# RWKV heads of a hybrid layer: the triangular inverse is multiplied into the removal keys and their output weights once per unit, and leaves the state chain

## The chip, the cores and the metric

The kernel runs on one NeuronCore of one Trainium2 chip. The metric is device time in microseconds (us) of one execution, median of several runs. All data is float32; the large products run on float32r pairs (a high and a low part, three products for one).

## What is computed

The reference is one layer of a hybrid trunk on a sequence of 2048 frames and 1024 channels: an RMS norm, one input projection of 4224 columns, three mixers side by side (RWKV-7 with 8 heads of 64, S5, RG-LRU), an output projection, a gated embedding and a last norm. The change touches the RWKV mixer alone. Cut to what matters, its reference is a recurrence over frames for each head:

```python
def step(S, inp):
    r_t, k_t, v_t, kk_t, b_t, d_t = inp
    S = (S * d_t[:, :, None, :]
         - jnp.einsum('bhvk,bhk->bhv', S, kk_t)[..., None] * b_t[:, :, None, :]
         + v_t[..., None] * k_t[:, :, None, :])
    return S, jnp.einsum('bhvk,bhk->bhv', S, r_t)
```

In a chunk of 64 frames the removals (the term with kk and b) depend on one another. Written for the whole chunk, the removed vectors are U = -M P. P is what the chunk's removal keys kk read from the old state and from the chunk's own values. M is the inverse of a unit lower triangular 64x64 matrix, made from the products of kk and b within the chunk and scaled by the norms of kk. U then enters the new state by its keys b and the output by its weights.

## The kernel before, in words

The sequence is worked through in two halves of 1024 frames. For each half there are 33 column tiles of the input projection, each in two blocks of 512 frames; one block is 8 x 3 matmuls of 128x128 by 128x512 (lines L332, L333, L334 in `inproj`, tile `ps_mm`). This is the feed. The RWKV work runs beside it, in 16 units (8 per half): a unit is a head pair, so two heads on the partitions 0 to 63 and 64 to 127, with two times 256 frames, in all 8 chunks of 64 (`NCH`).

A unit goes through three stages, written as Python generators. `rwkv_front` makes the keys and their products (`bk`, `kx`, `gr`, `mt`; matmuls L396, L398, L418 and L461; evictions on ScalarE and VectorE). `rwkv_solve` inverts the triangular matrices: 31 steps of two small VectorE operations (L80, `stmp` and `xs`) on all 32x32 blocks, a block transposition (L491, L497) into `tm`, and two rounds of 32x32 products (L530 and L541, tile `ps_late`), whose second eviction writes the off-diagonal block of `tm`. It also transposes `bk` into `kb` (L504, L506), makes the bonus (L511) and puts the centred values into `uv` (L519, evicted by two ScalarE copies, L523). `rwkv_chain` walks through the chunks, 4 steps of two chunks each, and carries the state.

One step of the chain before is three products in a row, each with an eviction behind it: (1) L570, `kx` times `uv`, gives P, which VectorE copies to `pt` (L577); (2) L585, `tm` times `pt`, gives U, evicted with a minus sign into `uv` by VectorE for one head and ScalarE for the other; (3) L592, `kb` times `uv`, is added to the state copy `sn` (L575, ScalarE) and scaled by VectorE into the next step's `uv`. Two products for the output (L581 from the old state, L603 from `uv` with the weights `gr`) go to `ps_y` beside them. The last step ends in a group norm (L611) and a store to `Yd`.

The order on TensorE (PE) is the order in which a loop at the end of the stage takes from the generators, and PE works strictly in that order. One tick of this loop takes 9 or 10 feed matmuls (`CHUNK_MM`), then one piece each of the chain, the solve and the front, up to their next `yield`; the number yielded says how many ticks that stage pauses. A front may begin every 15 ticks (`INTERVAL`). The other engines' orders are set by a list scheduler, in which chain, solve and front have the priorities 100, 50 and 0 (`PR_C`, `PR_S`, `PR_F`). The PSUM tiles matter too: `ps_prep` has two buffers, used by the front, by the normalised input's transposes (L319) and by L511; `ps_late` and `ps_chain` have one each.

After both halves the pools of this stage are closed, and the output projection (L922 to L924, `o1a`) and the S5 mixer begin. Their first loads (`st` from `w_out`, `st32` from `s5_a_re` and `s5_a_im`, L975) are issued on the one DMA queue of SyncE (SP), in order behind the last stores of the stage (`Yd` L356, `Gd` L707).

Of the kernel before, what the change touches and what calls it, by code (L numbers as in the profile page):

```python
# [12 lines left out]
AF = mybir.ActivationFunctionType  # L13
# [4 lines left out]
P = 128  # L18
# [4 lines left out]
C = 64  # L23
# [21 lines left out]
def hymba_layer(ctx: ExitStack, tc: tile.TileContext, x, p, norm_g, w_in,  # L45
# [83 lines left out]
    POOL.update((tag, rl) for tag in ("kx", "gr", "tm", "kb", "uv", "dl"))  # L129
    POOL.update((tag, rz) for tag in ("pt", "sn", "sp"))  # L130

# [338 lines left out]

    def rwkv_solve(n, v, mt, inv, bk, r):
        def wt(tag, shape=None, bufs=1):
            return pool_of(tag).tile(shape, F32, tag=tag, name=tag, bufs=bufs)
# [10 lines left out]
        for st in range(31):  # L484
# [4 lines left out]
            sub(xs[:, 0:ni, st + 1:32], xs[:, 0:ni, st + 1:32], tmp[:, 0:ni, 0:n])  # L489
        tn = wt("stmp", [P, 8, 32], 2).rearrange("p i (c q) -> p i c q", q=4)  # L490
        V.transpose(out=tn.rearrange("p i c q -> p i (c q)"), in_=xs)  # L491
        tm = wt("tm", [P, NCH, C], 2)
        for h in range(2):
            G.memset(tm[64 * h + 32:64 * h + 64, :, 0:32], 0.0)
            for bl in range(2):
                g = slice(64 * h + 32 * bl, 64 * h + 32 * bl + 32)
                V.transpose(out=tm[g, :, 32 * bl:32 * bl + 32], in_=tn[g].rearrange("p i c q -> p c i q"))  # L497

# [28 lines left out]
        for c in range(NCH):  # L527
            for h in range(2):
                o = 64 * h
                T.matmul(out=psc[o + 32:o + 64, 32 * c:32 * c + 32], lhsT=mt[o:o + 32, c, 32:64],  # L530
                         rhs=tn[o:o + 32, :, c], start=True, stop=True, tile_position=(o, o + 32))
        qn = wt("stmp", [P, 8, 32], 2)
# [5 lines left out]
        for c in range(NCH):  # L538
            for h in range(2):
                o = 64 * h  # L540
                T.matmul(out=psd[o:o + 32, 32 * c:32 * c + 32], lhsT=qn[o + 32:o + 64, c],  # L541
                         rhs=tm[o + 32:o + 64, c, 32:64], start=True, stop=True, tile_position=(o + 32, o))
        for h in range(2):
            hs = slice(64 * h, 64 * h + 32)
            act(tm[hs, :, 32:64], psd[hs, 0:256].rearrange("p (c t) -> p c t", t=32), AF.Copy, scale=-1.0)
        yield 1
        return tm, kb, uv, bon

    def rwkv_chain(pair, half, q, q_, gd):
        kx, gr, mt, inv, bk, r, dl, tm, kb, uv, bon = q_  # L550
        heads = [slice(0, 64), slice(64, 128)]
# [13 lines left out]
        for st in range(NS):  # L565
            cs = slice(st, NCH, NS)
            ps = psum.tile([P, 4, 2, C], F32, tag="chain", name="ps_chain", bufs=1)
            for j, c in enumerate((st, st + NS)):
                for h, hs in enumerate(heads):
                    T.matmul(out=ps[hs, 0, j], lhsT=kx[:, c, h], rhs=uv[:, c, h], start=True, stop=True,  # L570
                             tile_position=(0, 64 * h))
            if st > 0:
                sn = wt("sn", [P, 2, C], 2)
                for h, hs in enumerate(heads):
                    A.copy(out=sn[hs], in_=uv[hs, cs, h])  # L575
            pt = wt("pt", [P, 2, C])
            V.tensor_copy(out=pt, in_=ps[:, 0])  # L577
            yield W_C
            for c in (st, st + NS):
                for h, hs in enumerate(heads):  # L580
                    T.matmul(out=psy[hs, c * C:(c + 1) * C], lhsT=uv[hs, c, h], rhs=kx[hs, c, 2], start=(c == 0), stop=False,  # L581
                             tile_position=(64 * h, 64 * h), skip_group_check=True)
            for j, c in enumerate((st, st + NS)):
                for h, hs in enumerate(heads):
                    T.matmul(out=ps[hs, 1, j], lhsT=tm[hs, c], rhs=pt[hs, j], start=True, stop=True,  # L585
                             tile_position=(64 * h, 64 * h))
            ts(uv[heads[0], cs, 0], ps[heads[0], 1], -1.0, ALU.mult)
            act(uv[heads[1], cs, 1], ps[heads[1], 1], AF.Copy, scale=-1.0)
            yield 1
            for j, c in enumerate((st, st + NS)):  # L590
                for h, hs in enumerate(heads):
                    T.matmul(out=ps[hs, 2, j], lhsT=kb[:, c, hs], rhs=uv[:, c, h], start=True, stop=True,  # L592
                             tile_position=(0, 64 * h))
            sp = wt("sp", [P, 2, C])
            add(sp, ps[:, 2], sn)
            if st + 1 < NS:
# [260 lines left out]
    def solve_stage():  # L857
        for n, (half, pair, q) in enumerate(units):
            while len(fronts) <= n:
                yield 0  # L860
            yield from need(2, half, pair)
            v = load_z(2, q, zds[half][pair])
            f = fronts[n]
            solved.append(f + (yield from rwkv_solve(n, v, *f[2:6])))
            if n % 8 == 7 and half + 1 < NH:
                while len(chained) < n:
                    yield 0
                nxt[half + 1].append(fetch_x(half + 1, 1))
# [546 lines left out]
```

## Time and profile before

| what | value |
|---|---|
| median of 3 runs | 1825.19 us (1819.2 to 1825.2) |
| the profiled execution | 1823.06 us, of which the span from first to last instruction is 1821.3 us |
| mean granted TensorE clock in it | 0.989 |
| busy: PE matmul, VectorE, ScalarE, GpSimd | 96%, 71%, 53%, 2% of the span |
| DMA | 184.71 MB, mean 101 GB/s |
| feed and RWKV stage | from the start to about 1156.7 us of the span |

The profile is of one execution. PE is the matmul engine, PEld its weight loads, DVE is VectorE, ACT is ScalarE, POOL is GpSimd, SP issues DMAs. A row of a timeline gives start and duration in us; matmuls overlap in time, so what one of them costs is read from the distance between starts. A float32 matmul of the program stands in the trace as two instructions; a float32r one (the feed) as one.

### The profile page before, as it was taken

The page shows a single profiled execution, that of the slowest core. Times are in us where ns is not written, and L with a number is a line of the kernel's source. Part 1 is how long each engine was busy: PE and PEld are TensorE (multiplying, and loading weights), DVE is VectorE, ACT ScalarE, POOL GpSimd, SP SyncE. Part 2 cuts the span into 40 slices and gives each one's busy share as a digit, 9 for nine tenths or more (in the row PEclk, how much of TensorE's full clock was granted, in tenths as well). Part 3 has the DMA queues.
Part 4 walks back from the last instruction along what each step waited for, and adds up shares of the span by engine and source line. Part 5 has one row for each costly group of instructions (what it writes and reads, how often), then busy time and mean ns, then how long its engine had stood idle before and what let it go on. Part 6 is the DMA issues. An engine that isn't in the chain of part 4 may idle for free. (4 is left out here: it accounts for less than half of the span.)

```text
span 1821.3 us, 30173 instructions
## 1 busy us (share of the span) xinstructions
PE 1747.5 (96%) x11212; PEld 1346.6 (74%) x11212; DVE 1287.9 (71%) x3219; ACT 968.8 (53%) x1857; POOL 43.7 (2%) x105
## 2 busy tenths in 40 slices
PE   5999999999998999999999999899999999999997
PEld 4877777777676777777776767678888778888886
DVE  6279788688887439888688885786875685555554
ACT  5345864575757445665558565666763452232222
POOL 1000000000000000000000000000000000000000
PEclk9999999999999999999999999999999999999999
DMA  4332323222223233123222121742334893223220
GB/s 147 116 108 79 93 78 99 90 61 77 83 71 100 82 116 112 52 86 101 82 80 67 51 69 38 197 142 98 110 105 119 221 311 143 85 92 110 78 73 35
DMA packets 214620, 184.71 MB, mean 101 GB/s; under 512 B 59253, under 2 KB 182474, under 8 KB 214474
## 3 DMA queue, kind: packets, MB, share of 16 engines
q1 hardware_dynamic: 214474, 182.79, 32.5%
q8 instruction: 88, 1.44, 0.3%
q14 instruction: 58, 0.48, 0.1%
HBM read 121.73 MB, written 59.83 MB: 100 GB/s over the span
## 5 line engine op out<-in xcount | busy, mean ns | idle before, releaser
L332 PE MATMUL ps_mm<-xh,whi 128*128 128x512 f32 x1056 | 463.0, 438 | 0.9 <-ACT whi L192 0.7
L333 PE MATMUL ps_mm<-xh,wlo 128*128 128x512 f32 x1056 | 416.3, 394 | 0.8 <-DVE wlo L80 0.8
L334 PE MATMUL ps_mm<-xl,whi 128*128 128x512 f32 x1056 | 416.5, 394 | 0.0
L332 PEld LDWEIGHTS ps_mm<-xh,whi 128*128 128x128 f32 x1056 | 200.0, 189 | 79.1 <-issue 31.3
L333 PEld LDWEIGHTS ps_mm<-xh,wlo 128*128 128x128 f32 x1056 | 200.6, 190 | 46.6 <-issue 13.0
L334 PEld LDWEIGHTS ps_mm<-xl,whi 128*128 128x128 f32 x1056 | 200.0, 189 | 45.2
L80 DVE TENSOR_TENSOR stmp<-xs,ms 128x60 f32<-128x60 f32 (+24 forms) x496 | 103.3, 208 | 11.6
L80 DVE TENSOR_TENSOR xs<-xs,stmp 128x60 f32<-128x60 f32 (+24 forms) x496 | 102.7, 207 | 11.5
L923 PE MATMUL ps_mm<-woh,yl 128*128 128x512 f32 x256 | 103.1, 403 | 2.0 <-DVE yl L98 2.0
L922 PE MATMUL ps_mm<-woh,yh 128*128 128x512 f32 x256 | 102.4, 402 | 0.5 <-ACT yh L101 0.4
L924 PE MATMUL ps_mm<-pgl,hh 128*128 128x512 f32 x256 | 101.1, 395 | 0.3 <-DVE pgl L80 0.3
L924 PE MATMUL ps_mm<-wol,yh 128*128 128x512 f32 x256 | 101.3, 396 | 0.0
L923 PE MATMUL ps_mm<-pgh,hl 128*128 128x512 f32 x256 | 101.0, 394 | 0.0
L922 PE MATMUL ps_mm<-pgh,hh 128*128 128x512 f32 x256 | 100.8, 394 | 0.0
L80 DVE TENSOR_TENSOR wlo<-wraw,whi 128x512 fp32r<-128x512 f32 x132 | 88.5, 683 | 14.0 <-ACT whi L192 13.6
L101 ACT ACT_TABLE_LOAD x74 | 94.9, 1283 | 1.3
L101 ACT ACTIVATE ftg<-ps_mm 128x512 f32<-128x512 f32 x32 | 19.1, 598 | 135.4 <-PE ps_mm L924 135.4
L98 DVE SCALAR_TENSOR_TENSOR z<-ps_mm,pc,z 128x511 f32<-128x511 f32 x48 | 35.8, 745 | 69.9 <-ACT z L101 69.8
L192 ACT CAST whi<-wraw 128x512 fp32r<-128x512 f32 x132 | 77.9, 614 | 0.7 <-DMA wraw<-in_w_in 0.2
L98 DVE SCALAR_TENSOR_TENSOR e<-ftg,e 128x1024 f32<-128x1024 f32 x16 | 19.6, 1226 | 78.1 <-ACT ftg L101 78.1
L101 ACT ACTIVATE uv<-ps_chain 64x128 f32<-64x128 f32 x64 | 17.4, 272 | 97.9 <-DVE uv L93 97.2
L101 ACT ACTIVATE z<-ps_mm,dc 128x512 f32<-128x512 f32 x48 | 32.8, 682 | 66.3 <-PE ps_mm L334 66.2
(332 smaller groups left out, 3535.9 us busy)
## 6 DMA issues: line engine op xcount, KB each, us to landing
wraw<-in_w_in SPq DMA_DIRECT2D x132, 256.0 KB
zd<-z SPq DMA_DIRECT2D x48, 256.0 KB
yr<-Yd SPq DMA_DIRECT2D x16, 512.0 KB
Hd<-ht SPq DMA_DIRECT2D x16, 512.0 KB
hr<-Hd SPq DMA_DIRECT2D x16, 512.0 KB
xr<-in_x SPq DMA_DIRECT2D x16, 512.0 KB
out<-e SPq DMA_DIRECT2D x16, 512.0 KB
st<-in_w_out SPq DMA_DIRECT2D x12, 512.0 KB
```

Source lines behind the costliest of these rows:

```text
L80: V.tensor_tensor(out=out, in0=a, in1=b, op=op)
L98: V.scalar_tensor_tensor(out=out, in0=a, scalar=s, in1=b, op0=op0, op1=op1)
L101: A.activation(out=out, in_=in_, func=func, scale=scale, bias=bias)
L192: A.copy(out=hi[:, ks], in_=raw)
L332: T.matmul(out=ps, lhsT=hi[:, k], rhs=xh, start=(k == 0), stop=False)
L333: T.matmul(out=ps, lhsT=lo[:, k], rhs=xh, start=False, stop=False)
L334: T.matmul(out=ps, lhsT=hi[:, k], rhs=xl, start=False, stop=(k == KD - 1))
L922: T.matmul(out=ps, lhsT=a_h[:, k], rhs=b_h[k][:, ns], start=(ends[0] and k == 0), stop=False)
L923: T.matmul(out=ps, lhsT=a_l[:, k], rhs=b_h[k][:, ns], start=False, stop=False)
L924: T.matmul(out=ps, lhsT=a_h[:, k], rhs=b_l[k][:, ns], start=False, stop=(ends[1] and k == nk - 1))
```

## The change

The solve stage now ends with one more piece, and the chain has two products in a row. With M in `tm`, the solve stage multiplies M into the removal keys (`kb`, 16 matmuls of 64x64 by 64x64) and into their output weights (`gr`, 16 more), line L553 after the change; both are written back in place, with a minus sign, by four ScalarE evictions of 64 partitions x 512. The chain then writes P itself into `uv` where U stood (VectorE for one head, ScalarE for the other), and the next product takes it with the new `kb` and `gr`. The products L581 are issued with L570 (L586 with L582 after the change), since P overwrites the state that they read; `pt` is gone. For these products M is needed in the other orientation, so the transposes behind the 31 steps change: three over 128 partitions x 256 in place of one such and four over 32 x 256, and the off-diagonal block is made at another place of `tm`.

```diff
-        tn = wt("stmp", [P, 8, 32], 2).rearrange("p i (c q) -> p i c q", q=4)
-        V.transpose(out=tn.rearrange("p i c q -> p i (c q)"), in_=xs)
         tm = wt("tm", [P, NCH, C], 2)
+        for bl in range(2):
+            V.transpose(out=tm[:, :, 32 * bl:32 * bl + 32].rearrange("p c (i q) -> p i c q", q=4), in_=xs)
+        t1 = wt("stmp", [P, 8, 32], 2)
+        V.transpose(out=t1, in_=tm[:, :, 32:64])
         for h in range(2):
-            G.memset(tm[64 * h + 32:64 * h + 64, :, 0:32], 0.0)
-            for bl in range(2):
-                g = slice(64 * h + 32 * bl, 64 * h + 32 * bl + 32)
-                V.transpose(out=tm[g, :, 32 * bl:32 * bl + 32], in_=tn[g].rearrange("p i c q -> p c i q"))
+            G.memset(tm[64 * h:64 * h + 32, :, 32:64], 0.0)
...
-                T.matmul(out=psd[o:o + 32, 32 * c:32 * c + 32], lhsT=qn[o + 32:o + 64, c],
-                         rhs=tm[o + 32:o + 64, c, 32:64], start=True, stop=True, tile_position=(o + 32, o))
+                T.matmul(out=psd[o + 32:o + 64, 32 * c:32 * c + 32], lhsT=t1[o + 32:o + 64, c],
+                         rhs=qn[o + 32:o + 64, c], start=True, stop=True, tile_position=(o + 32, o + 32))
...
         yield 1
-        return tm, kb, uv, bon
+
+        for ps, of in ((plate(), lambda hs, h: kb[hs, :, hs]), (pprep(), lambda hs, h: gr[hs, :, h])):
+            for c in range(NCH):
+                for h in range(2):
+                    hs = slice(64 * h, 64 * h + 64)
+                    T.matmul(out=ps[hs, c * C:(c + 1) * C], lhsT=tm[hs, c], rhs=of(hs, h)[:, c], start=True, stop=True,
+                             tile_position=(64 * h, 64 * h))
+            for h in range(2):
+                hs = slice(64 * h, 64 * h + 64)
+                act(of(hs, h), ch(ps)[hs], AF.Copy, scale=-1.0)
+        yield 1
+        return kb, uv, bon
...
+            for c in (st, st + NS):
+                for h, hs in enumerate(heads):
+                    T.matmul(out=psy[hs, c * C:(c + 1) * C], lhsT=uv[hs, c, h], rhs=kx[hs, c, 2], start=(c == 0), stop=False,
+                             tile_position=(64 * h, 64 * h), skip_group_check=True)
             if st > 0:
                 sn = wt("sn", [P, 2, C], 2)
                 for h, hs in enumerate(heads):
                     A.copy(out=sn[hs], in_=uv[hs, cs, h])
-            pt = wt("pt", [P, 2, C])
-            V.tensor_copy(out=pt, in_=ps[:, 0])
+            V.tensor_copy(out=uv[heads[0], cs, 0], in_=ps[heads[0], 0])
+            A.copy(out=uv[heads[1], cs, 1], in_=ps[heads[1], 0])
             yield W_C
-            for c in (st, st + NS):
-                for h, hs in enumerate(heads):
-                    T.matmul(out=psy[hs, c * C:(c + 1) * C], lhsT=uv[hs, c, h], rhs=kx[hs, c, 2], start=(c == 0), stop=False,
-                             tile_position=(64 * h, 64 * h), skip_group_check=True)
             for j, c in enumerate((st, st + NS)):
                 for h, hs in enumerate(heads):
-                    T.matmul(out=ps[hs, 1, j], lhsT=tm[hs, c], rhs=pt[hs, j], start=True, stop=True,
-                             tile_position=(64 * h, 64 * h))
-            ts(uv[heads[0], cs, 0], ps[heads[0], 1], -1.0, ALU.mult)
-            act(uv[heads[1], cs, 1], ps[heads[1], 1], AF.Copy, scale=-1.0)
-            yield 1
-            for j, c in enumerate((st, st + NS)):
-                for h, hs in enumerate(heads):
-                    T.matmul(out=ps[hs, 2, j], lhsT=kb[:, c, hs], rhs=uv[:, c, h], start=True, stop=True,
+                    T.matmul(out=ps[hs, 1, j], lhsT=kb[:, c, hs], rhs=uv[:, c, h], start=True, stop=True,
                              tile_position=(0, 64 * h))
```

Three places of the order, first on PE. A chain step before, between the feed's own rows (`ps_mm`); `uv` holds the state and the values, `ps_chain` the step's products:

```order
L570 MATMUL ps_chain<-uv,kx 64x64 x4
L332 MATMUL ps_mm<-xh,whi 128x512
...
L334 MATMUL ps_mm<-xl,whi 128x512
L581 MATMUL ps_y<-kx,uv 64x64 x4
L585 MATMUL ps_chain<-pt,tm 64x64 x4
L332 MATMUL ps_mm<-xh,whi 128x512
...
L334 MATMUL ps_mm<-xl,whi 128x512
L592 MATMUL ps_chain<-uv,kb 64x64 x4
L603 MATMUL ps_y<-gr,uv 64x64 x4
```

The same step after the change (L582, L586, L597, L608 are L570, L581, L592, L603):

```order
L582 MATMUL ps_chain<-uv,kx 64x64 x4
L586 MATMUL ps_y<-kx,uv 64x64 x4
L332 MATMUL ps_mm<-xh,whi 128x512
...
L334 MATMUL ps_mm<-xl,whi 128x512
L597 MATMUL ps_chain<-uv,kb 64x64 x4
L608 MATMUL ps_y<-gr,uv 64x64 x4
```

The step has two pieces where it had three; the output product from the old state moved up to the first of them.

The end of a solve on PE after the change, in a unit where a front's products (L461) fall in the same tick; L542 is the 32x32 product that was L541:

```order
L542 MATMUL ps_late<-stmp 32x32 x16
L332 MATMUL ps_mm<-xh,whi 128x512
...
L334 MATMUL ps_mm<-xl,whi 128x512
L553 MATMUL ps_late<-kb,tm 64x64 x16
L553 MATMUL ps_prep<-gr,tm 64x64 x16
L461 MATMUL ps_prep<-kx,bk 128x128 x8
```

Before the change the solve ended with the first of these rows. The two rows of L553 are new, and L461 uses the buffers of `ps_prep` behind the second of them.

The four new evictions on ACT, in one of these units:

```order
L101 ACTIVATE kk<-zk,pc 128x256 x2
L101 ACTIVATE kb<-ps_late 64x8x64 x2
L101 ACTIVATE sq<-kk 128x512
L101 ACTIVATE gr<-ps_prep 64x8x64 x2
L466 COPY mt<-ps_prep 32x256
L466 COPY mt<-ps_prep 32x4x32
```

None of the rows of `kb` and `gr` was there before; here a piece of the next front (`sq`) stands between them, and the evictions of L461's products (`mt`) come behind them.

The end of the stage on SP, before:

```order
L104 DMA st<-in_w_out 128x1024 x2
L356 DMA Yd<-rst 128x2x128 x2
L975 DMA st_12706<-in_s_a_re 32x64
L707 DMA Gd<-g_12650 128x512
L975 DMA st_12706<-in_s_a_re 32x64
L975 DMA st_12706<-in_s_a_im 32x64 x2
L104 DMA st<-in_w_out 128x1024 x3
```

And after, where L980 is L975 and L712 is L707; the last `Yd<-rst` store stands 13 rows further up and isn't among these:

```order
L104 DMA st<-in_w_out 128x1024
L980 DMA st_12898<-in_s_a_re 32x64 x2
L980 DMA st_12898<-in_s_a_im 32x64
L712 DMA Gd<-g_12842 128x512
L980 DMA st_12898<-in_s_a_im 32x64
L104 DMA st<-in_w_out 128x1024
```

The last store of the RWKV stage and most weight loads moved ahead of the last gate store; one of the four small loads still stands behind it.

More of the change, by code (lines that the diff above doesn't have):

```diff
@@ L129, in hymba_layer @@
     POOL.update((tag, rl) for tag in ("kx", "gr", "tm", "kb", "uv", "dl"))
-    POOL.update((tag, rz) for tag in ("pt", "sn", "sp"))
+    POOL.update((tag, rz) for tag in ("sn", "sp"))
     def pool_of(tag):
@@ L469, in rwkv_front, with rwkv_solve @@
         return kx, gr, mt, inv, bk, r, dl
-    def rwkv_solve(n, v, mt, inv, bk, r):
+    def rwkv_solve(n, v, gr, mt, inv, bk, r):
         def wt(tag, shape=None, bufs=1):
@@ L530, in rwkv_solve @@
                 T.matmul(out=psc[o + 32:o + 64, 32 * c:32 * c + 32], lhsT=mt[o:o + 32, c, 32:64],
-                         rhs=tn[o:o + 32, :, c], start=True, stop=True, tile_position=(o, o + 32))
+                         rhs=tm[o:o + 32, c, 0:32], start=True, stop=True, tile_position=(o, o + 32))
         qn = wt("stmp", [P, 8, 32], 2)
@@ L540, in rwkv_solve @@
                 o = 64 * h
-                T.matmul(out=psd[o:o + 32, 32 * c:32 * c + 32], lhsT=qn[o + 32:o + 64, c],
-                         rhs=tm[o + 32:o + 64, c, 32:64], start=True, stop=True, tile_position=(o + 32, o))
+                T.matmul(out=psd[o + 32:o + 64, 32 * c:32 * c + 32], lhsT=t1[o + 32:o + 64, c],
+                         rhs=qn[o + 32:o + 64, c], start=True, stop=True, tile_position=(o + 32, o + 32))
         for h in range(2):
-            hs = slice(64 * h, 64 * h + 32)
-            act(tm[hs, :, 32:64], psd[hs, 0:256].rearrange("p (c t) -> p c t", t=32), AF.Copy, scale=-1.0)
+            hs = slice(64 * h + 32, 64 * h + 64)
+            act(tm[hs, :, 0:32], psd[hs, 0:256].rearrange("p (c t) -> p c t", t=32), AF.Copy, scale=-1.0)
         yield 1
-        return tm, kb, uv, bon
+        for ps, of in ((plate(), lambda hs, h: kb[hs, :, hs]), (pprep(), lambda hs, h: gr[hs, :, h])):
[9 more added lines that the diff above has]
+        return kb, uv, bon
     def rwkv_chain(pair, half, q, q_, gd):
-        kx, gr, mt, inv, bk, r, dl, tm, kb, uv, bon = q_
+        kx, gr, mt, inv, bk, r, dl, kb, uv, bon = q_
         heads = [slice(0, 64), slice(64, 128)]
@@ L575, in rwkv_chain @@
                     A.copy(out=sn[hs], in_=uv[hs, cs, h])
-            pt = wt("pt", [P, 2, C])
-            V.tensor_copy(out=pt, in_=ps[:, 0])
+            V.tensor_copy(out=uv[heads[0], cs, 0], in_=ps[heads[0], 0])
+            A.copy(out=uv[heads[1], cs, 1], in_=ps[heads[1], 0])
             yield W_C
-            for c in (st, st + NS):
-                for h, hs in enumerate(heads):
-                    T.matmul(out=psy[hs, c * C:(c + 1) * C], lhsT=uv[hs, c, h], rhs=kx[hs, c, 2], start=(c == 0), stop=False,
-                             tile_position=(64 * h, 64 * h), skip_group_check=True)
             for j, c in enumerate((st, st + NS)):
                 for h, hs in enumerate(heads):
-                    T.matmul(out=ps[hs, 1, j], lhsT=tm[hs, c], rhs=pt[hs, j], start=True, stop=True,
-                             tile_position=(64 * h, 64 * h))
-            ts(uv[heads[0], cs, 0], ps[heads[0], 1], -1.0, ALU.mult)
-            act(uv[heads[1], cs, 1], ps[heads[1], 1], AF.Copy, scale=-1.0)
-            yield 1
-            for j, c in enumerate((st, st + NS)):
-                for h, hs in enumerate(heads):
-                    T.matmul(out=ps[hs, 2, j], lhsT=kb[:, c, hs], rhs=uv[:, c, h], start=True, stop=True,
+                    T.matmul(out=ps[hs, 1, j], lhsT=kb[:, c, hs], rhs=uv[:, c, h], start=True, stop=True,
                              tile_position=(0, 64 * h))
             sp = wt("sp", [P, 2, C])
-            add(sp, ps[:, 2], sn)
+            add(sp, ps[:, 1], sn)
             if st + 1 < NS:
@@ L863, in solve_stage @@
             f = fronts[n]
-            solved.append(f + (yield from rwkv_solve(n, v, *f[2:6])))
+            solved.append(f + (yield from rwkv_solve(n, v, *f[1:6])))
             if n % 8 == 7 and half + 1 < NH:
```

## The prediction, made before the run

> **What bounds the kernel now.** I read the page, then the busy time by stage, then the waits of PE, then single intervals of the timeline. Engines and stages first (columns: window, its length, busy time with instruction count of PE, PEld, DVE, ACT and POOL, granted clock, DMA share, GB/s):
>
> ```profile
> span 1821.3 us, 30173 instructions
> PE 1747.5 (96%) x11212; PEld 1346.6 (74%) x11212; DVE 1287.9 (71%) x3219; ACT 968.8 (53%) x1857; POOL 43.7 (2%) x105
> ...
> 0.00:1156.70 1156.70, 1108.74 (x8322) 825.90 (x8322) 865.39 (x2523) 689.24 (x1398) 22.33 (x69) 0.99 0.29 87
> ...
> 100.00:560.00 460.00, 450.77 (x3514) 333.13 (x3511) 381.26 (x1142) 286.75 (x583) 7.03 (x19) 0.99 0.28 83
> ...
> 690.00:1110.00 420.00, 409.13 (x3404) 301.14 (x3403) 351.68 (x1075) 253.51 (x512) 3.67 (x12) 1.00 0.25 75
> ```
>
> The change lies wholly in the first 1156.7 us. In the two stretches where RWKV units run, PE is idle for 460.0 - 450.8 = 9.2 and 420.0 - 409.1 = 10.9 us, about 2%. DVE is at 83%, ACT at 60 to 62%. PE is the bound there: a product that is added to it costs its full time, and a wait that disappears can give back no more than these idle stretches. Which waits they are (waits of PE up to 1160 us and from 560 to 600 us; us in total, times, longest):
>
> ```profile
> PE ps_prep L461 <- DVE gr L80: 3.2, 2, 2.5
> PE ps_chain L592 <- ACT uv L101: 2.9, 6, 0.8
> PE ps_y L581 <- DVE rst L80: 2.4, 3, 1.4
> PE ps_chain L570 <- DVE uv L80: 1.0, 2, 0.9
> ...
> PE ps_prep L319 <- DVE xl L98: 5.7, 4, 3.1
> ```
>
> The state chain is hardly waited for: L570, L581 and L592, the three places where a step takes up an eviction, cost 6.3 us together over 64 steps. Nine feed matmuls between two pieces of the chain cover its evictions. The chain is no critical path that could be shortened; its third product only takes PE time.
>
> **The change part by part.** What a small group costs on PE is read from the starts of the feed matmuls around it.
>
> ```profile
> 522.57 0.39 PE L334 MATMUL ps_mm<-xl,whi 128*128 128x512 f32 x1
> 522.88 0.45 PE L570 MATMUL ps_chain<-uv,kx 128*64 128x64 f32 x8
> 523.26 0.50 PE L332 MATMUL ps_mm<-xh,whi 128*128 128x512 f32 x1
> 523.60 0.39 PE L333 MATMUL ps_mm<-xh,wlo 128*128 128x512 f32 x1
> 523.83 0.40 PE L334 MATMUL ps_mm<-xl,whi 128*128 128x512 f32 x1
> ...
> 589.40 0.39 PE L334 MATMUL ps_mm<-xl,whi 128*128 128x512 f32 x1
> 589.72 0.45 PE L581 MATMUL ps_y<-kx,uv 64*64 64x64 f32 x8
> 590.00 0.40 PE L585 MATMUL ps_chain<-pt,tm 64*64 64x64 f32 x8
> 590.33 0.50 PE L332 MATMUL ps_mm<-xh,whi 128*128 128x512 f32 x1
> 590.67 0.39 PE L333 MATMUL ps_mm<-xh,wlo 128*128 128x512 f32 x1
> ...
> 1077.66 0.39 PE L334 MATMUL ps_mm<-xl,whi 128*128 128x512 f32 x1
> 1077.98 0.45 PE L570 MATMUL ps_chain<-uv,kx 128*64 128x64 f32 x8
> 1078.36 1.15 PE L519 MATMUL ps_late<-cen,zv 64*64 64x64 f32 x32
> 1079.43 0.50 PE L332 MATMUL ps_mm<-xh,whi 128*128 128x512 f32 x1
> 1079.77 0.40 PE L333 MATMUL ps_mm<-xh,wlo 128*128 128x512 f32 x1
> ```
>
> Undisturbed feed starts lie 0.23 apart (523.60 to 523.83). From L334 over a gap to the L333 behind it is two such steps, 0.46. With 8 small instructions in the gap it is 523.60 - 522.57 = 1.03, a delay of 0.57; with 16 it is 590.67 - 589.40 = 1.27, a delay of 0.81. So 8 instructions cost 0.24, 0.030 each, and the interruption of the feed itself 0.57 - 0.24 = 0.33. With 8 + 32 it is 2.11, a delay of 1.65, where 40 x 0.030 + 0.33 = 1.53 would be due: the missing 0.12 stands at the change of shape, since from L570 (128 rows) to the next start is 0.38, from L581 to L585 (both 64 rows) 0.28. I take 0.10 for such a change.
>
> 1. Removed: L585, 64 groups of 8 instructions: 64 x 0.24 = -15.4 us.
> 2. Added: 32 products per unit, 64 instructions in the trace; 16 x 64 x 0.030 = +30.7 us. They have exactly the shape of L585 and L519.
> 3. Interruptions: counted in the order of PE, the feed is broken 285 times before and 266 times after, since a step takes two ticks and not three, while the solve takes one more and its pieces now less often fall together with one of the chain. 19 x 0.33 = -6.3 us.
> 4. L586 now follows L582 in one group, with a change of shape inside it: 64 x 0.10 = +6.4 us (0 if the switch hides elsewhere).
>
> PE alone thus has 30.7 + 6.4 - 15.4 - 6.3 = +15.4 us more, between +9 and +17.
>
> At this place the Trainium skill speaks for the change: TensorEngine Tiling (Array Packing), section Key Properties, says that changing the tiling mode drains the TensorE. The trace agrees (0.33 for an interruption, 0.10 for a change of shape within one); by that rule alone, without the products, the edit would gain the 6.3 us and lose the 6.4.
>
> 5. A new wait. The order of PE shows `ps_prep` products of L461 in the same tick behind the new ones in 10 of the 16 units. `ps_prep` has two buffers: the new product takes one, the first four products of L461 the other, and the next four need the first again, so they wait for the evictions of `gr`, which stand on ACT behind those of `kb`. What an ACT eviction of this size costs and how late it comes:
>
> ```profile
> L523 ACT COPY uv<-ps_late 64x512 f32<-64x512 f32 x32 | 18.5, 579 | 16.4 <-PE ps_late L519 16.1
> ...
> L461 PE MATMUL ps_prep<-kx,bk 64*128 64x128 f32 x512 | 56.4, 286 | 3.4 <-DVE gr L80 3.2 <-PE ps_late L541 0.2
> ...
> 407.77 1.15 PE L519 MATMUL ps_late<-cen,zv 64*64 64x64 f32 x32 [0.65 <-ACT kb L506]
> ...
> 409.68 0.63 ACT L101 ACTIVATE lth<-lth 128x512 f32<-128x512 f32 x1
> 410.34 1.17 ACT L523 COPY uv<-ps_late 64x512 f32<-64x512 f32 x2
> ```
>
> When the `kb` products end, PE has the 32 instructions for `gr` (0.95) and four of L461 (56.4 / 64 = 0.88, with 0.1 for the shape): 1.93 us. ACT needs four evictions, 4 x 0.579, and about 0.1 of latency: 2.42. So PE waits at least 0.5 us. Late evictions add to it: here L519 ended at 408.92 and its eviction began 1.42 later, behind a table load and an activation. Most begin at once, but in ACT's new order other work stands between the `kb` and `gr` evictions in five of the ten units. I take 1.1 us: 10 x 1.1 = +11, between +5 and +25. Behind the waiting L461 stand the feed itself and, on ACT and DVE, the evictions of that front piece.
>
> 6. Chain waits: the one at L581 goes (-2.4); those at L592 and L570 have the same cover of nine feed matmuls, and the evictions are of the same size (64 x 128 on each engine). A new order inside: P may overwrite the state only after L586 and the `sn` copies; both end before the copy would start anyway. I take -2.4, between -5 and +3.
> 7. VectorE and ScalarE.
>
> ```profile
> L577 DVE COPY pt<-ps_chain 128x128 f32<-128x128 f32 x64 | 18.0, 281 | 23.2 <-PE ps_chain L570 22.9
> L497 DVE STREAM_TRANSPOSE tm<-stmp 32x256 f32<-32x256 f32 x64 | 27.8, 435 | 1.2
> ```
>
> DVE loses one of two evictions per step, 18.0 us, and four transposes per unit for two more of the same free size, 27.8 - 32 x 0.435 = 13.9 us: 32 us of 865 in the stage. DVE is not the bound; of the waits on it above (3.2 and 5.7) I take half, -4, between -9 and 0. ACT gains 64 evictions x 0.579 = 37 us at about 61% load: nothing but what item 5 counts.
>
> 8. The end of the stage. The last group norm product (L611) has 33 feed matmuls behind it before and 114 after. What stands there now:
>
> ```profile
> 1156.28 0.39 PE L334 MATMUL ps_mm<-xl,whi 128*128 128x512 f32 x1
> 1161.66 0.28 PE L1008 MATMUL ps_prep<-ident,st 32*128 32x32 f32 x1 [4.99 <-DMA st<-in_s_a_re]
> ...
> 1156.81 0.89 SPq L356 DMA_DIRECT2D Yd<-rst  x2
> ...
> 1158.43 0.37 SPq L707 DMA_DIRECT2D Gd<-g  x1
> 1158.84 0.44 SPq L975 DMA_DIRECT2D st<-in_s_a_re  x1
> 1159.33 0.89 SPq L975 DMA_DIRECT2D st<-in_s_a_im  x2
> ```
>
> SP holds the small loads back behind the last `Yd` store, and that store comes early after the change. But in the new order of SP one of the four `st` loads still stands behind the last `Gd` store, which needs the end of the feed; it moves up by three issues at most, about 1 us, and the weights, now loaded earlier, save some of the slow start behind it. -3, between -6 and 0.
>
> Sum: 15.4 + 11 - 2.4 - 4 - 3 = +17. The profiled execution took 1823.06 us (span 1821.3), 2.1 below the median of the runs and inside their spread; 1823.06 + 17 = 1840.
>
> **The rivals.** *Waits fall more than the products cost (faster).* If the DVE work that goes and the shorter chain took away the waits whole, that is 6.3 (chain), 3.2 and 5.7 (DVE) and 5 at the end, 20 us, against 9 (item 1 to 4 at its low end) and the least new wait, 5: 1823 - 6 = 1817, and with hidden waits inside busy PE time perhaps 1812. For it: DVE at 83% is close behind PE. Against: a sum of idle PE time so small. It decides where products cost under 0.02 us each. Chance 0.09.
>
> *The balance (no change).* Products at the low end of +9, the new wait at +5, gains of -9: 1828. Chance 0.21.
>
> *The clock (slower than forecast).* PE loses its clock behind poorly filled stretches (columns: window, length, PE busy, granted clock, DMA share, GB/s):
>
> ```profile
> 510.30:513.70 3.40, 2.18 (x44) 1.00 0.09 10
> 513.70:517.10 3.40, 3.40 (x16) 0.50 0.55 173
> ```
>
> PE worked 2.18 of 3.40 us here, part of it in 32x32 products, and ran at 0.50 for the next 3.40 us: 1.7 us lost. The new tick is 1.9 us of 64x64 products, 1.8 of L461 and the wait between, about 5 us without feed; if each of the ten lost 1.7 us, that is 17 more: 1857. Against: 64x64 products run in pairs on both halves of the rows, and long ticks without a wait kept the clock. Chance 0.12. The Trainium skill, TensorE: Matmul & The Clock Gate, section on the HAM clock gate, says that the gate looks at PE's activity in free-running windows of 3413 ns; the trace agrees in the 3.40 us steps.
>
> *The chain is not shorter in time.* Fronts begin every 15 ticks whatever the chain takes, and in PE's order the fronts' L418 stand at the same feed positions (288, 420, 561, 711, ...) before and after. This is part of the forecast: the shorter chain ends a unit earlier, but starts the next no sooner.
>
> **How the numbers follow.** Forecast 1840 with chance 0.58; the clock 0.12; the balance 0.21; faster 0.09. The range takes in the lower bound of the balance at about 1826 and the clock case at 1857. 0.5% is 9.1 us, about what a measurement of this kernel can tell from no change; slower by more is forecast and clock, 0.70.
>
> **What would show it.** L553 as 1024 instructions with some 32 us between feed starts; waits of L461 for ACT `gr`, about 1 us each in ten units; L577 and L585 gone; PE idle time near 1157 down to about 4 us; no stretch in which the chain is waited for. It is wrong if the stage ends at 1157 us or before (now 1156.7, forecast about 1176), or if L461 does not wait.

## The result, and the profile after

The changed kernel takes 1889.65 us (median of 4 runs, 1887.37 to 1892.36) against 1823.2 before: a ratio of 1.0368 with a 95% interval of 1.034 to 1.0396. It is slower, as forecast, but by 66 us where 17 were forecast, and outside the range.

The top of the page of the changed kernel, and then its windows view, cut at the last feed matmul (same columns as before):

```profile
span 1885.6 us, 31245 instructions
PE 1782.0 (95%) x11724; PEld 1383.8 (73%) x11724; DVE 1270.8 (67%) x3123; ACT 1005.5 (53%) x1920; POOL 44.0 (2%) x105
```

```profile
0.00:1217.50 1217.50, 1138.43 (x8834) 858.31 (x8834) 852.05 (x2430) 729.37 (x1464) 22.62 (x69) 0.97 0.28 84
1217.50:1885.60 668.10, 643.53 (x2891) 525.49 (x2890) 418.77 (x694) 276.11 (x457) 21.37 (x36) 0.98 0.39 124
```

The stage ends at 1217.5 where it ended at 1156.7: 60.8 us of the 64.3 by which the span grew. In it PE is idle 1217.5 - 1138.4 = 79.1 us (before 1156.7 - 1108.7 = 48.0), 31 more. Its busy time grew by 29.7. Part of that is work at half clock: the trace's clock records show PE busy for 59.8 us at a granted clock of 0.5 in this stage, before 23.9. Counted as half lost, the difference is 18.0 us. The other 11.8 are work at full clock. So 31 us are waits, 18 the clock, 12 the work. The prediction's sum had, in this stage, 11 for new waits less 6.4 for old ones, nothing for the clock, and 15.4 for the work.

The waits of PE up to 1230 us (us in total, times, longest):

```profile
PE ps_prep L461 <- DVE bk L80: 20.6, 7, 6.6
PE ps_mm L332 <- ACT la L101: 11.0, 4, 6.4
PE ps_prep L319 <- DVE xt L93: 8.4, 5, 2.9
PE ps_prep L461 <- ACT gr L101: 5.7, 7, 2.2
PE ps_mm L669 <- ACT li L101: 4.8, 2, 4.2
...
PE ps_prep L1013 <- DMA st<-in_s_a_re: 4.5, 1, 4.5
...
PE ps_prep L553 <- ACT nrow L420: 3.2, 1, 3.2
```

L461 waits for `gr` on ScalarE, as forecast, with 5.7 us. But the first line was not in the trace of before and is in no step of the prediction: L461, the front's own products, comes to PE before VectorE has made their input `bk`. The second and the fifth line are waits for ScalarE's evictions of `la` and `li`, gates of the RG-LRU mixer whose products stand in the feed. They were small before:

```profile
PE ps_mm L664 <- ACT li L101: 0.5, 1, 0.5
PE ps_mm L332 <- ACT la L101: 0.2, 1, 0.2
```

These 15 us more are in no step of the prediction either. Of the runs below, no_products has them too (11.5 and 4.8), without one new product, and bk_wait_5 less (5.0 and 0.9); but `la` is as long in gate_late_two_ticks (12.9), where L461 is late. What holds up these two evictions isn't shown.

One place of the first kind, in rows of PE, ACT and DVE (start, duration, in brackets the idle time ahead):

```profile
795.95 1.15 PE L553 MATMUL ps_late<-kb,tm 64*64 64x64 f32 x32
...
798.09 0.47 ACT L101 ACTIVATE ta<-ps_prep,dc 128x256 f32<-128x256 f32 x1
798.45 1.19 ACT L101 ACTIVATE kb<-ps_late 64x512 f32<-64x512 f32 x2
799.64 0.57 ACT L420 COPY nrow<-ps_prep 2x512 f32<-2x512 f32 x1
800.27 1.97 PE L553 MATMUL ps_prep<-gr,tm 64*64 64x64 f32 x32 [3.17 <-ACT nrow L420]
802.57 1.18 ACT L101 ACTIVATE gr<-ps_prep 64x512 f32<-64x512 f32 x2
...
803.77 1.28 ACT L101 ACT_TABLE_LOAD   x1
805.06 0.47 ACT L101 ACTIVATE ta<-ps_prep,dc 128x256 f32<-128x256 f32 x1
805.57 0.69 DVE L98 SCALAR_TENSOR_TENSOR b<-ta,kk 128x512 f32<-128x512 f32 x1
805.57 0.60 ACT L101 ACTIVATE km<-ta,dc 128x256 f32<-128x256 f32 x1
...
808.71 0.69 DVE L98 SCALAR_TENSOR_TENSOR bk<-b,einv 64x512 f32<-64x512 f32 x1
808.82 3.37 PE L461 MATMUL ps_prep<-kx,bk 64*128 64x128 f32 x16 [6.58 <-DVE bk L80]
...
812.12 0.79 PE L332 MATMUL ps_mm<-xh,whi 128*128 128x512 f32 x1
```

The front's `nrow` and the second halves of its `ta` and `km` stand on ScalarE behind the new evictions (and a table load), `bk` comes after them, and PE stands still for 3.17 and 6.58 us with no feed in between. The new evictions are not what makes `bk` late, though: at the same place in the order PE waits 7.46 us for `bk` in no_products and 6.01 in no_evictions (both below), which have none of them. PE runs at half clock here: the 32 instructions for `gr` take 1.97 where those for `kb` took 1.15, and 16 of L461 take 3.37 where they took 1.71 before the change (at 458.18).

Why L461 is early is told by the order, not by the trace. The second half of a front stands in the code behind `while len(chained) < n - 1: yield 0`, a gate that the end of a chain opens. The shorter chain opens it earlier. In the order of PE the fronts' L418 stand where they stood (but for one of sixteen), but L461 moved up: in the first half its first tick in a front stood at feed matmul 642, 780, 960, 1098, 1272, 1404 before (third to eighth unit), and stands at 612, 750, 900, 1050, 1194, 1335 now. From L418 to L461 it was 69 to 120 feed matmuls in these units, and now is 36 to 51. In the first two units of each half nothing moved: L461 stands 36 to 42 behind L418 in both kernels, and there it doesn't wait for `bk`. No chain runs beside these fronts yet. So the distance alone doesn't make the wait; that it depends on what else the engines have to do is likely, but not shown.

### The profile page after: what moved, and what is told of

It is laid out like the page before. It is cut to its first block, busy times and chain, and to the rows that moved or that the text cites. A ratio compares the mean times of both kernels' runs of the same rounds, so it can differ in the third digit from the quotient of the medians.

```text
span 1885.6 us, 31245 instructions
## 1 busy us (share of the span) xinstructions
PE 1782.0 (95%) x11724; PEld 1383.8 (73%) x11724; DVE 1270.8 (67%) x3123; ACT 1005.5 (53%) x1920; POOL 44.0 (2%) x105
## 5 line engine op out<-in xcount | busy, mean ns | idle before, releaser
L461 PE MATMUL ps_prep<-kx,bk 64*128 64x128 f32 x512 | 68.3, 307 | 26.9 <-DVE bk L80 20.6
L461 PEld LDWEIGHTS ps_prep<-kx,bk 64*128 64x128 f32 x512 | 60.2, 208 | 34.4 <-issue 13.1
```

The lines of the kernel that those rows point to most:

```text
L461: T.matmul(out=ps[:, q * P:(q + 1) * P], lhsT=bk[hs, c].rearrange("p a t -> p (a t)"), rhs=kx[hs, c, h:3:2 - h], start=True, stop=True)
```

## The experiments

Theory A: the early gate costs the time; L461 reaches PE before `bk`, and the clock falls behind the holes (a hole is a wait in which PE stands still). Rival B: the new products and their evictions do it by themselves. The order of a kernel is summed up by two distances in feed matmuls: from a front's L418 to its L461 (third to eighth unit of each half), and from its last L461 to the next front's first product L396 (number of the 14 places below 24, the turn of the halves left out). Ratios are to the kernel before, run beside it.

| kernel | us | ratio, 95% interval | L418 to L461 | close L396 |
|---|---|---|---|---|
| before | 1823.2 | 1 | 63 to 120 | 2 |
| the change | 1889.65 | 1.0368 (1.034 to 1.0396) | 36 to 51 | 0 |
| no_products | 1850.26 | 1.0167 (1.0151 to 1.0183) | as the change | 0 |
| no_evictions | 1868.86 | 1.0268 (1.0248 to 1.0289) | as the change | 0 |
| gate_late | 1863.21 | 1.0228 (1.0209 to 1.0247) | 72 to 147 | 6 |
| gate_late_no_products | 1813.15 | 0.9953 (0.9924 to 0.9982) | as gate_late | 6 |
| gate_late_no_evictions | 1850.03 | 1.0145 (1.013 to 1.016) | as gate_late | 6 |
| gate_late_two_ticks | 1877.24 | 1.0293 (1.0275 to 1.031) | 87 to 153 | 6 |
| before_bk_wait_0 | 1894.35 | 1.0389 (1.0373 to 1.0404) | 27 to 57 | 0 |
| bk_wait_5 | 1834.12 | 1.0064 (1.0047 to 1.0081) | 72 to 111 | 2 |
| bk_wait_5_no_products | 1793.61 | 0.9841 (0.9821 to 0.9861) | as bk_wait_5 | 2 |
| bk_wait_5_split | 1827.58 | 1.0033 (1.0016 to 1.0051) | as bk_wait_5 | 2 |
| bk_wait_6 | 1869.51 | 1.0266 (1.0238 to 1.0294) | 90 to 135 | 8 |
| before_bk_wait_5 | 1872.17 | 1.0273 (1.025 to 1.0296) | 90 to 159 | 10 |
| gate_late_front_pause | 1853.91 | 1.0184 (1.0163 to 1.0205) | 72 to 126 | 0 |
| before_bk_wait_5_front_pause | 1853.29 | 1.0186 (1.016 to 1.0213) | 75 to 138 | 0 |
| before_front_pause | 1815.12 | 0.9969 (0.9956 to 0.9982) | 63 to 120 | 0 |
| bk_wait_5_split_front_pause | 1827.64 | 1.0044 (1.0024 to 1.0065) | 72 to 111 | 0 |

### Gate and products, each with and without

gate_late puts the gate back near its old place; the front's gate then asks for `opened` in place of `chained`:

```diff
-        while len(chained) < n - 1:
+        while len(opened) < n - 1:
...
             ended.append(n)
+            yield 2
+            opened.append(0)
```

> All of the change, but the next front's gate opens four ticks later, so that the front's products (L461) stand about where they stood before the change. Theory A (the shorter chain opened the gate early, and the front's products now reach PE before VectorE has made bk): the waits of L461 and most of the half-clock time go, and what is left is the added PE work, so about 1840 us. Rival B (the new products and their evictions themselves hold up PE and ScalarE, wherever the front stands): stays above 1870 us.

The `yield 2` also pauses the chain stage for two ticks. That is not what gate_late costs: bk_wait_6, further below, has no such pause, and in the last two units of the first half its L461 (1299 and 1434) and its chains (1464 and 1581) begin at the same feed matmuls; it is no faster.

no_products leaves out the loop with L553 and its evictions and keeps the empty tick, so `kb` and `gr` stay without the inverse; P is multiplied by 0. no_evictions leaves out only the `act` lines of that loop, with P times 0 as well. gate_late_no_products is the first two together.

> The change without its two groups of products and their four evictions; the piece of the solve that held them is empty, fronts stand as after the change. It leaves out the multiplication by the inverse, and P is written into uv times zero to stay finite. Theory A: PE loses about 39 us of products, but L461 still comes too early and waits for bk: 1835 to 1855 us. Rival B: all of the loss goes and L585's 15 us with it: 1800 to 1820 us.

> The change with the products on PE, but without the four ScalarE evictions that write them back (P into uv times zero to stay finite). Theory A: the evictions are not the cause, above 1870 us. Rival B in its ScalarE form (ta, km and nrow of the front stand behind the evictions on ScalarE): PE keeps its products, the waits go, about 1835 to 1845 us.

> Both: the gate four ticks later and no products and evictions (P into uv times zero). Both theories: the kernel before less the removed product, 1800 to 1815 us; with the three others it tells whether gate and products add up (A and B separate causes) or only hurt together.

The four corners, all beside 1819.7 for the kernel before in this batch: the early gate costs 1850.3 - 1813.2 = 37 us without any new product (the four runs of the second scatter by 13.6 us). In no_products L461 waits for `bk` as it does after the change:

```profile
PE ps_prep L461 <- DVE bk L80: 27.9, 8, 7.5
PE ps_mm L332 <- ACT la L101: 11.5, 5, 6.4
```

and in no_evictions, with the products but without their evictions, nearly as long:

```profile
PE ps_prep L461 <- DVE bk L80: 21.2, 11, 6.0
```

In gate_late L461 has no wait for `bk`. Theory A holds for that half. But gate_late took 1863, between theory A's 1840 and the 1870 of rival B: products and evictions cost 50 us with the late gate (1863.2 - 1813.2) and 36 to 39 with the early one (1850.3 to 1886.7 = 1819.7 x 1.0368, or to 1889.7), where 42 were forecast. Read the other way, the early gate costs only 23 to 26 us with the products in place. no_evictions (two runs) stands 18.6 above no_products and some 18 to 21 below the change: products and evictions share the price about equally there. Its 1868.9 lies just under the 1870 that theory A asked for and far above rival B's 1845.

### The early place alone, and the late place by another way

before_bk_wait_0 changes one number of the kernel before; bk_wait_5 the same number of the changed kernel:

```diff
-W_LOAD, W_Z, W_BK, W_SOLVE, W_GN, W_C = 2, 1, 3, 8, 1, 1
+W_LOAD, W_Z, W_BK, W_SOLVE, W_GN, W_C = 2, 1, 0, 8, 1, 1
```

> The kernel before, with one number changed: the front's pause W_BK between the VectorE work on bk and the products L461 that read it is 0 ticks and not 3. No product is added and the chain keeps its three products. L461 then stands where it stands after the change (feed matmuls 612, 750, 912, 1050, 1203, 1335 against 612, 750, 900, 1050, 1194, 1335; before the change 642, 780, 960, 1098, 1272, 1404). Theory A (L461 comes to PE before VectorE has made bk, and that alone is worth the 37 us between no_products and gate_late_no_products): 1845 to 1860 us, with waits of L461 for bk of 20 us or more. Rival B (the place of L461 is harmless, it hurts only with the new products and their evictions on ScalarE, or with a shorter chain): 1815 to 1828 us.

> The whole change, with the gate as the change has it, and W_BK 5 in place of 3: the front's work on VectorE begins as early as after the change, its products L461 stand where gate_late has them (651, 792, 960, 1098 against 651, 792, 981, 1116). Theory A (only the distance between bk and L461 counts): as gate_late or a little less, 1852 to 1866 us, no waits of L461 for bk. Rival B (the early start of the front's VectorE and ScalarE work is what disturbs, since it falls on the solve's evictions): above 1875 us.

In the first no product is added, the chain is as long as ever, and the kernel loses 71.6 us, more than by the whole change. That is also more than theory A's 1845 to 1860. The number moves L461 in all units, not only in those in which the change moves it: in the first two of each half it stands 18 to 21 behind L418 where it stood 36 to 42, and 14 of the 23 us of waits for `bk` are there. By feed position (the end of the feed matmul of the same number) these units cost 26 of 73 us at the feed's end; the other 47 fall where L461 stands about as after the change. Its waits of PE up to 1250 us begin like those after the change:

```profile
PE ps_prep L461 <- DVE bk L80: 23.4, 9, 7.0
PE ps_mm L332 <- ACT la L101: 14.1, 5, 4.9
PE ps_prep L461 <- DVE gr L80: 9.1, 6, 2.6
```

bk_wait_5 is the whole change with L461 two ticks later. It takes 1834.1, 11 us above the kernel before; 55 of the 66 us are gone. Its stage up to the last feed matmul (the profiled execution took 1827.0, the shortest of the four):

```profile
0.00:1162.80 1162.80, 1111.69 (x8834) 842.67 (x8834) 836.57 (x2428) 728.83 (x1463) 22.15 (x69) 0.99 0.29 87
```

PE is idle 51.1 us (before 48.0), the clock is 0.99 again, and `bk` is not among the waits. Against the change the stage is 54.7 us shorter: 28.0 us of idle time, 21.5 of the clock (PE is busy at half clock for 16.8 us, not 59.8) and 5.3 of full-clock work. The last has a reason of its own: in this order more pieces fall into the same tick, and the feed is broken (interrupted by other work) 245 times, not 265. The time lies under even the low end of what theory A expected: 1834 instead of 1852. What gate_late loses beside it (1.0228 - 1.0064 of 1822.8, 30 us) is not the distance from L418 to L461, which is no shorter there.

### Where the products' price lies

gate_late_two_ticks puts a `yield 1` between the products for `kb` and those for `gr`; gate_late_no_evictions leaves out the evictions.

> gate_late with the new products in two ticks: the 16 for kb, nine feed matmuls, the 16 for gr. The four evictions on ScalarE stay. gate_late lies 50 us above its version without the products. Theory C (of these 50 about 31 are the products on PE as predicted, and the rest comes from the four evictions in a row, which hold back gr, the second ps_prep buffer and the front's ScalarE work): 1848 to 1857 us, no waits of L461 for gr. Rival D (a product costs PE 50 ns in place of 30, and a second interruption adds 16 times 0.33): 1863 to 1870 us.

> gate_late with the new products on PE but without their evictions (kb and gr stay without the inverse, P is multiplied by 0 so that the values stay finite). Theory C (PE pays 31 us for the products, the evictions the other 19): 1840 to 1848 us. Rival D (PE pays all of the 50 for the products): 1858 to 1865 us. Rival E (nearly all comes from the evictions): 1813 to 1830 us.

Theory C falls with two_ticks, and rival D's 1863 to 1870 is missed too: from 300 us on L461 waits 1.7 us for `gr` on ScalarE where it waited 4.0 in gate_late, yet by the ratios the kernel became 12 us slower, not 10 faster. The extra tick also moved L461 further back (last but one column). Its first waits show what came in their place:

```profile
PE ps_mm L332 <- ACT la L101: 12.9, 6, 6.3
PE ps_prep L319 <- DVE xt L93: 12.8, 7, 2.8
PE ps_prep L396 <- DVE xs L80: 7.8, 2, 5.2
```

By the ratios gate_late_no_evictions lies 15 us under gate_late and 35 over gate_late_no_products, between C and D. Comparing arrangements that all lose time elsewhere did not settle the price; the next batch has it where little else is lost.

> bk_wait_5 without the new products and their evictions (kb and gr stay without the inverse, P is multiplied by 0 so that the values stay finite). It tells what products and evictions cost where nothing else is disturbed; the prediction had 30.7 for the products and 11 for the wait that their evictions make, 42 together. Theory A: 1834 minus 32 to 45, 1789 to 1802 us. Rival B (as with the gate late, 50 or more): below 1785 us.

With W_BK 5 products and evictions cost 1834.1 - 1793.6 = 40.5 us, inside theory A's 32 to 45; the prediction had 30.7 + 11 = 42. By the accounting used above, full-clock work in the stage is 1066.6 without and 1103.3 with them, 36.7 us for the products (forecast 30.7). And it was 1096.8 before: what falls away is worth 30.2 us of PE, where the prediction had 15.4 + 6.3 - 6.4 = 15.3. Much of both differences is breaks of the feed, at the prediction's 0.33 us each: there are 284 before, 245 in bk_wait_5 and 235 without the products. So 10 breaks, 3.3 us, stand in the 36.7, and 49 breaks, 16.2 us, in the 30.2, where 19 were counted. Only 19 of the 49 are the change's own (it has 265); 20 come with W_BK 5 and 10 with leaving out the products.

> bk_wait_5 with the four evictions of the new products shared: for each product group the first head's goes to VectorE, the second's to ScalarE, where both went to ScalarE in a row. Theory A (the waits of L461 for gr, 7.9 us in bk_wait_5, come from four evictions in a row on one engine; two and two take half as long): 1820 to 1830 us, waits of L461 for gr below 4 us. Rival B (VectorE in the solve is the tighter engine, and its own work comes later): 1834 to 1850 us.

```diff
-                act(of(hs, h), ch(ps)[hs], AF.Copy, scale=-1.0)
+                if h:
+                    act(of(hs, h), ch(ps)[hs], AF.Copy, scale=-1.0)
+                else:
+                    ts(of(hs, h), ch(ps)[hs], -1.0, ALU.mult)
```

1827.6, within theory A's 1820 to 1830: some 6 us less, with waits of L461 for `gr` on ScalarE down from 7.9 to 4.7 (theory A had asked for less than 4), though on VectorE they rose from 0.6 to 2.8. The runs of bk_wait_5 and this one scatter by 10 and 12 us, so the size of the gain is not sharp.

### Too late is also wrong

> The whole change with W_BK 6. L461 stands one tick later than in bk_wait_5 (672, 810, 990, 1122 against 651, 792, 960, 1098), near its places in gate_late. Theory A (beyond the distance that bk needs, more only draws the units out): 1832 to 1862 us, not faster than bk_wait_5. Rival B (5 is still too short, as the waits of L461 for ScalarE gr, 7.9 us, may say): 1815 to 1828 us.

> The kernel before with W_BK 5 in place of 3, for a like comparison with bk_wait_5. L461 then stands later than before (681, 822, 1020, 1152 against 642, 780, 960, 1098) and from the sixth unit on the fronts begin later too (1050 against 1011). Theory A (the kernel before already leaves bk enough time, so more distance gives nothing, and the units are drawn out as in gate_late): 1825 to 1850 us, slower than before. Rival B (the kernel before also loses time to bk, and the comparison with bk_wait_5 was not a fair one): 1795 to 1812 us.

One tick more costs bk_wait_6 35 us, and two ticks more cost the kernel before 49. Both lie above what theory A expected, 1869.5 over 1862 and 1872 far over 1850. Five is not too short, and more distance is not harmless. Waits that bk_wait_6 has:

```profile
PE ps_mm L332 <- ACT la L101: 7.3, 5, 2.2
PE ps_prep L398 <- ACT s L101: 5.4, 3, 1.9
...
PE ps_prep L418 <- DVE bon L80: 4.9, 2, 2.7
```

The last two lines are the next front's first products. Fronts run one after another, so where L461 is late, the next front's L396 stands right behind it (last column of the table). The four runs that follow put `yield 2` at the end of each front in `front_stage`; L461 keeps its place, only the next front starts later.

> The kernel before with the pause of two ticks between fronts and nothing else. Only two of its fronts follow directly (6 and 9 feed matmuls behind L461); they now come 24 and 27 behind. Theory F: a few us less, 1812 to 1820 us. Rival G: 1820 to 1827 us.

> gate_late with a pause of two ticks between the end of one front and the start of the next. L461 stands where it stands in gate_late; the next front's first product L396 comes 27 feed matmuls or more behind it, where it was 6 to 21 in eight of the fifteen places. Theory F (a front that follows directly on the last front's products meets their evictions on ScalarE and VectorE, and its own first products then wait): 1825 to 1842 us. Rival G (the units lie later, into the second half's norm and the end of the stage, and that is what costs): 1858 to 1868 us as in gate_late.

> before_bk_wait_5 with the same pause of two ticks between fronts. L461 keeps its late places (681, 822, 1020, 1152); L396 comes 24 feed matmuls or more behind, where it was 9 to 21 in ten of the fifteen places. Theory F (directly following fronts): 1820 to 1842 us. Rival G (the late place of the units): 1866 to 1878 us as in before_bk_wait_5.

> bk_wait_5_split (the whole change, W_BK 5, the new evictions shared by VectorE and ScalarE) with the pause of two ticks between fronts. Two of its fronts follow at 18 feed matmuls; they now come 27 behind. Theory F: 1818 to 1827 us. Rival G: 1825 to 1832 us. Whether the change brings anything when both kernels are set well is told by this run against before_front_pause: the prediction's +15 for PE alone would leave it 5 to 15 us behind.

(The second of these counts eight close places in gate_late; there are six.) In before_front_pause, at 1815.1 and below both kernels, the theory of the directly following front (F) is seen at one place. First PE in the kernel before, where L396 follows L461 (at 458.18) after six feed matmuls, then the windows around it:

```profile
462.54 0.40 PE L585 MATMUL ps_chain<-pt,tm 64*64 64x64 f32 x8
462.87 1.13 PE L396 MATMUL ps_prep<-zl,wla 64*128 64x256 f32 x4
465.49 1.67 PE L398 MATMUL ps_prep<-zl,wla 64*128 64x256 f32 x4 [1.49 <-DVE stmp L80]
...
469.39 0.63 PE L333 MATMUL ps_mm<-xh,wlo 128*128 128x512 f32 x1
469.81 0.63 PE L334 MATMUL ps_mm<-xl,whi 128*128 128x512 f32 x1
```

```profile
462.00:465.50 3.50, 2.01 (x23) 1.25 (x21) 3.47 (x11) 2.52 (x7) 0.00 (x0) 1.00 0.00 0
465.50:472.30 6.80, 6.80 (x14) 4.30 (x15) 4.58 (x16) 3.99 (x8) 0.00 (x0) 0.53 0.00 0
```

The same front in before_front_pause, and the same windows (the whole lies 0.6 us earlier):

```profile
465.67 0.40 PE L603 MATMUL ps_y<-gr,uv 128*64 128x64 f32 x8
...
470.51 1.13 PE L396 MATMUL ps_prep<-zl,wla 64*128 64x256 f32 x4
471.83 1.13 PE L398 MATMUL ps_prep<-zl,wla 64*128 64x256 f32 x4 [0.20 <-DVE bon L80]
```

```profile
462.00:465.50 3.50, 3.50 (x26) 2.27 (x22) 3.38 (x13) 2.10 (x5) 0.00 (x0) 1.00 0.00 0
465.50:472.30 6.80, 6.60 (x49) 4.55 (x50) 6.52 (x22) 6.57 (x12) 0.00 (x0) 1.00 0.31 82
```

A wait of 1.49 us of PE is followed by 6.8 us at about half clock, in which feed matmuls start 0.42 apart and not 0.23. By feed position the two kernels run level up to matmul 1260 (0.6 us apart), differ by 6.8 us at 1320, and by 8.8 at the end of the feed.

For the late kernels the directly following front is a part only: by the ratios gate_late gains 8 us and before_bk_wait_5 16, and both stay above the 1842 that theory F allowed. 22 us of gate_late over bk_wait_5 and 34 of before_bk_wait_5 over the kernel before are left where the fronts no longer follow directly. By feed position gate_late_front_pause is ahead of bk_wait_5 by up to 14 us in the first half (at 1113), 7.0 behind after that half's units (at 1740) and 21.5 at the feed's end, with PE at half clock for 23 us more of busy time (39.9 against 16.8). Which work meets there, another mixer's, the second half's norm or the solve, was not tried and stays open. And where only two fronts followed at 18, in bk_wait_5_split, the pause brought nothing: 1827.6 both times, by the ratios 2 us more, at the edge of theory F's range and inside rival G's.

With both kernels at the best settings tried, 1827.6 stands against 1815.1 on the same chip: there the change is about 12 us slower, within the 5 to 15 expected. Better settings for either are not ruled out.

## Why the prediction was wrong, point by point

- **The step that failed is the rival "the chain is not shorter in time", taken into the forecast**: "Fronts begin every 15 ticks whatever the chain takes", with L418 at the same feed positions. That is true of L418 (but for one), and says nothing of the front's other half: L461 stands behind the gate that the chain opens, and from the third unit of each half on it moved up by 27 to 78 feed matmuls. With it the chains themselves begin 18 to 69 feed matmuls sooner, against "starts the next no sooner". The forecast read one line of a stage and took it for the stage. So its sum had no term for waits on `bk` (20.6 us measured), none for those on `la` and `li` (15 more) and none for the clock (18). The gate by itself costs 37 us without the new products, and with L461 set back (bk_wait_5) the change costs 11, near the 17 of the forecast. That nearness is in part luck, for W_BK 5 also saves 20 breaks of the feed.
- **What bounds the kernel**: PE, but "a wait that disappears can give back no more than these idle stretches" reads in one direction only. That PE was idle for 2% where units ran did not say how close below it VectorE and ScalarE were in order and time: from the third unit of a half on they had `bk` ready in time with 63 feed matmuls or more, and often not with 36 to 51.
- **Item 1 to 4 (PE +15.4, between +9 and +17)**: right in sum; full-clock work rose by 11.8. The count of breaks was right as well (284 to 265 in the traces). The sizes show in bk_wait_5 only together with its own breaks: the products cost 36.7 for 30.7, of which 3.3 are breaks, and 30.2 fall away for 15.3, of which 16.2 are breaks and some 5 stay unexplained.
- **Item 5 (waits of L461 for `gr`, +11 between +5 and +25)**: right in mechanism, 5.7 us in seven places after the change, 7.9 in six in bk_wait_5. The new evictions also stand ahead of the front's `ta` and `km` (rows at 798 to 806 us), but the waits for `bk` are there without them.
- **Item 6 (chain waits, -2.4)**: waits of L582 and L597 are 0.4 and 1.4 us after the change; the chain stayed uncritical.
- **Item 7 (VectorE 32 us less in the stage, ScalarE 37 more)**: the sizes were right. The rows of L577 and of the transposes are 33 us less after the change, and ACT rose by 36.7. (The page's busy time of DVE fell by only 17.1, in bk_wait_5 by 30.0.) The waits on VectorE that it named did fall, by more than 4 us: L461 for `gr` from 3.2 to 0.7, L319 for `xl` from 8.2 to 4.2. The 20.6 for `bk` outweigh that.
- **Item 8 (the end of the stage, -3)**: the wait for `st` fell by half a us (4.99 to 4.49), but what follows the feed took 668.1 us and not 664.6, 3.5 longer, with PE busy at half clock for 20.1 us there against 7.3.
- **The clock**: named as a rival at 0.12 and +17, at the ticks of the new products. Its price was near, 18 us in the stage, its place was not: of the 59.8 us at half clock 23 follow waits for `bk` alone, 10 one for `nrow` and then one for `bk`, 14 the long waits for `la` and `li`, 6 one for `gr`. And it is there in no_products too (69.4 us of busy time at half clock, without one new product). That the price came out near is luck. The Trainium skill, TensorE: Matmul & The Clock Gate, in the section on the HAM clock gate, gives an idle window of about 3.4 us as what throttles PE. Here a window in which PE was busy for 2.01 of 3.50 us sufficed (at 462, shown above), so the wait to watch for is shorter than that.
- **What would show it**: the prediction asked for a stage end of about 1176; at 1217 it should have been read as wrong, and in bk_wait_5 it is 1162.8. Both of its signs of being wrong, a stage end at 1157 or before and no wait of L461, look to the fast side; neither came, though it was wrong on the slow one.

## What to carry to other kernels

When work is interleaved by hand, a shorter stage moves everything that waits for its end. Before pricing a change, list for every gate, buffer or counter that it touches what stands behind it, and compare for each consumer on the bounding engine the distance to its producer before and after; the start of a stage does not stand for its end. And when a change loses more than its work, turn the spacing constants of both kernels before judging it: here one tick too many cost 35 us, two 49, and three too few 72, more than the edit's own 12.

## What the runs showed of the hardware

One short hole on PE can cost several times its length in a kernel that PE bounds. The wait of 1.49 us at 464 cost 6.2 us by feed position (0.6 at matmul 1260, 6.8 at 1320); the clock stood near one half for the next 6.8 us, which explains about half of that. Not every such hole does it: in the same stage of the same kernel waits of 1.50, 1.25, 1.41 and 1.32 us (at 478, 595, 782 and 990) were followed by no half clock. In this trace's clock records the starts of half clock lie whole multiples of 3.41 us apart, so where a hole falls between these steps may decide; that was not tried. Over the stage, before_bk_wait_0 was idle for 40 us more than the kernel before and lost another 36 to the clock (95.1 us of busy time at half clock against 23.9, half of the difference).
